# A hybrid decoder trunk on one core: a new plan for the first attention with five single PSUM banks and doubled keys, weights ahead of rows in the second mixer, and shorter reciprocal roots

## The chip, the cores and the metric

The kernel runs on one core of one Trainium2 chip. The metric is the device time of one execution in microseconds (us), the median over several runs; lower is better.

## The reference

The trunk has two layers on a residual stream `h` of 1024 tokens by 1024 features, all float32. Each layer is a token mixer and a channel mixer, each behind an RMS norm and added to `h`. Layer 0 mixes tokens by forgetting attention (16 heads of 64, causal, with a cumulated log-sigmoid gate as a bias), layer 1 by native sparse attention over keys and values that are computed once from `h` after layer 0. The channel mixer is a gated MLP (1024 to 2 x 2816 to 1024) with a causal convolution of width 3.

```python
def rms_norm(x, g):
    y = xf * lax.rsqrt(jnp.mean(xf * xf, axis=-1, keepdims=True) + RMS_EPS)
    return (y * g.astype(jnp.float32)).astype(x.dtype)
...
def forgetting_attention(xn, w_in, b_f, q_gain, k_gain, w_out):
    proj = xn @ w_in
    q = rms_norm(proj[..., :HD].reshape(B, T, N_HEADS, HEAD_DIM), q_gain)
    k = rms_norm(proj[..., HD:2 * HD].reshape(B, T, N_HEADS, HEAD_DIM), k_gain)
    v = proj[..., 2 * HD:3 * HD].reshape(B, T, N_HEADS, HEAD_DIM)
    c = jnp.cumsum(log_f, axis=1).transpose(0, 2, 1)
    ...
        s = jnp.einsum('bhqd,bhkd->bhqk', qb, k) * scale
        s = s + cb[..., :, None] - c[..., None, :]
        s = jnp.where(kpos[None, :] <= qpos[:, None], s, -jnp.inf)
        p = jax.nn.softmax(s, axis=-1)
        return jnp.einsum('bhqk,bhkd->bqhd', p.astype(v.dtype), v)
    ...
    return o @ w_out
...
    for layer in range(DEPTH):
        if layer < N_A_LAYERS:
            h = h + forgetting_attention(rms_norm(h, a_norm[i]), ...)
        else:
            h = h + native_sparse_attention(rms_norm(h, b_norm[i]), positions, kc, vc, ks, vs, kw, vw, ...)
        h = h + conv_ffn(rms_norm(h, f_norm[layer]), f_w_up[layer], f_conv_w[layer], f_conv_b[layer], f_w_down[layer])
        if layer == N_A_LAYERS - 1:
            kv = shared_kv(h, positions, ...)
```

## The kernel before

Matmuls run on operands that are split in a high and a low part (`_h`, `_l`, 128 x 512 pieces): ACT casts the high part, DVE or POOL subtracts it from the source for the low part (lines L894 and L895, L1102 and L1098), and a product is three matmuls (L220, L221, L222: high by high, low by high, high by low).

The stages, in order of time: input projections of layer 0 (to about 247 us); the first attention (to about 612 us); the rest of its output projection (648); the first mixer, `ffn0` (1291); the inputs of the second attention, `nsa_in` (1470); the second attention, `nsa` (2008); the second mixer, `ffn1`.

Within a stage each engine works its instructions off in the order of the program. That order is set when the program is built, by a planner (`Flow`): each step is a task with an engine, an estimated duration, a due time `u` and a letter; the table `PLAN` gives each letter a shift of its due time. The planner simulates the engines with the estimated durations and takes at each point the ready task that is due first. A `ready` holds a task back to a time on the planner's clock. A ring is a set of buffers that tasks take and give back.

A step of the first attention, for a head and one or two tiles of 128 queries: PE multiplies queries by keys into a score tile (L627, `s`); DVE reads it, adds the mask and finds the maximum (L635, `pt`, `sm`); ACT takes the exponential (L637); DVE inverts the row's sum (L640); POOL scales the row (L641); PE transposes blocks of 128 (L654, `t`); ACT casts the high part (L665, `p_h`); DVE subtracts for the low part (L667, `p_l`); PE multiplies by the values (L659, L660, `v`). Between these stand the late products (queries, keys and values of the second half of the heads, for the last four tiles; products of `w_h`, `wo_h` and `w_raw` into `t`), the loads and splits of the output weights (`wo_h`, `wo_l`, from `w_raw<-in_a_w_out`), and an early part of the output projection.

PSUM's eight banks are given out so in this stage: three single ones to the ring `t`, four to the ring `s` (two score tiles of two banks), one to `v`:

```python
        ring("t", 3, [P, 512], FT, space=PSUM, ordered=False)
        ring("s", 2, [P, T], FT, space=PSUM)
        ring("v", 1, [P, 512], FT, space=PSUM)
```

Queries and keys go through DRAM. A key tile is stored as 64 rows high and 64 rows low for each head (`s_k`, L494 and L762), and loaded as `ka` (the high rows twice, by two DMAs of 64 rows) and `kb` (the low rows and two rows of the gate, L802). All these DMAs are issued by SP, in order.

An RMS norm's reciprocal root is five DVE operations around two of ACT (L253 `tensor_scalar`, L245 `Ln`, L246 `Exp`, L249 to L252 one Newton step). In `ffn0` the function `leave` takes each finished row tile: square with sum (ACT, L2228), root, scaling on POOL (L2231), transposes.

At the start of `ffn1` three last row tiles are loaded, squared (L1170), scaled on POOL (L1172) and transposed (L1183), while the first weights are cast (L1102) and their lows are subtracted on DVE (L1098).

Of the kernel before, what the change touches and what calls it, by code (L numbers as in the profile page):

```python
# [16 lines left out]
P = 128  # L17
# [33 lines left out]
def moved(*shape):  # L51
# [5 lines left out]
    "fox": dict(F=1e3, G=-11.5, R=.5, M=5, E=-1, K=-.5, H=-1.5, L=-5.5, V=2, J=-4, D=1.5, N=18.5, Q=1.5, W=13, P=-3, S=0, O=1, spread=.7, wo=.6, wo_from=21, side=2, late=2, step=1.6, gap=.015),  # L57
# [3 lines left out]
    "nsa": dict(D=18.5, E=28, F=40.5, G=42.5, H=3, J=17, K=19, L=-5.5, M=20, N=-11.5, O=15, P=19.5, Q=6.5, R=20, S=-1, V=28.5, W=25.5, none=18.5, spread=0.3, wo=3, wo_from=2, side=2, cmp=0.5, gap=0.05, load=1.2),  # L61
# [40 lines left out]
class Flow:  # L102
# [3 lines left out]
    def __init__(self, plan):  # L106
        self.plan, self.rings, self.tasks = plan, {}, []
# [41 lines left out]
    def run(self):  # L149
        free = {t.eng: 0.0 for t in self.tasks}  # L150
# [46 lines left out]
class Trunk:  # L197
# [34 lines left out]
    def rstd(self, pool, ss, n, inv, p=P):  # L232
        steps, r = self.rstd_steps(pool, ss, n, inv, p)
        for f in steps:
            f()
        return r

    def rstd_steps(self, pool, ss, n, inv, p=P, room=None):
# [5 lines left out]
        def root():  # L244
            nc.scalar.activation(y, v, AF.Ln)  # L245
            nc.scalar.activation(y, y, AF.Exp, scale=-0.5)  # L246

        def correct():
            nc.vector.tensor_mul(t, y, y)  # L249
            nc.vector.tensor_mul(t, t, v)  # L250
            nc.vector.tensor_scalar(t, t, -0.5, 1.5, op0=OP.mult, op1=OP.add)
            nc.vector.tensor_mul(r, y, t)  # L252
        return (lambda: nc.vector.tensor_scalar(v, ss, inv, EPS, op0=OP.mult, op1=OP.add), root, correct), r  # L253

    def rstd_tasks(self, ss, n, inv, scale, room=lambda: None):
# [3 lines left out]
        def begin():  # L259
            st["f"], st["r"] = self.rstd_steps(self.ap_o, ss(), n, inv, room=room())  # L260
            st["f"][0]()

        def end():
            st["f"][2]()
            scale(st["r"])
        return [("DVE", .08, "Q", begin), ("ACT", .36, "Q", lambda: st["f"][1]()), ("DVE", 1.42, "Q", end)]
# [33 lines left out]
    def zeros(self, cp):  # L300
        nc = self.nc
        one_zero = cp.tile([P, 2], FT, name="one_zero")
        self.one, self.zero = one_zero[:, :1], one_zero[:, 1:]
# [118 lines left out]
    def fox_in(self, cp, xT, qT, kT, vS, extras, room):  # L422
        nc, A = self.nc, self.A
        w_in = A["a_w_in"][0]
        with self.pool("fi_s", 2) as sp, self.pool("fi_w", 2) as wp, \
# [12 lines left out]
            def gate():  # L438
# [37 lines left out]
                for x, c in enumerate((ch, cl)):  # L476
                    nc.sync.dma_start(kT[:, :, 2 * HD + x, :].rearrange("p a t -> (p a) t"), f32(c))

            def spill(o, dst, half, i, gain):
# [12 lines left out]
                for x, t in enumerate((hi, lo)):  # L492
                    for a in range(2):
                        nc.sync.dma_start(dst[4 * half:4 * half + 4, a, x * HD:(x + 1) * HD, tl].rearrange("p d t -> d p t"),  # L494
                                          f32(t[a * HD:(a + 1) * HD]))
# [1841 lines left out]
```

## Time and profile before

| | |
|---|---|
| median of 3 runs | 2655.86 us (2654.89 to 2657.86) |
| profiled execution | 2656.26 us, span 2654.5 us |
| busy PE / PEld / DVE | 2590.8 (98%) / 2165.1 (82%) / 2158.6 (81%) |
| busy ACT / POOL | 1523.1 (57%) / 541.6 (20%) |
| DMA | 310.80 MB, mean 117 GB/s |

Busy times are sums over the span and can hide in one engine's wait for another; PE's records overlap, since a matmul is started before the last one has ended. The stage is what the profile is read by.

### The profile page before, as it was taken

How to read it: one execution, taken by the hardware profiler on the slowest of the kernel's cores; microseconds unless marked ns; L12 is line 12 of the kernel's file. 1: busy time of each engine (PE TensorE's matmuls, PEld its weight loads, DVE VectorE, ACT ScalarE, POOL GpSimd, SP SyncE). 2: the span in 40 equal slices, each digit the busy share in tenths (PEclk: the TensorE clock that was granted, in tenths of full speed). 3: DMA queues.
4: the chain of work that ended last, by engine and by line, in shares of the span. 5: the costliest groups of instructions: out<-in, count | busy, mean ns of one | idle time of the engine just before them, and what ended most of it. 6: DMA issues, size and time to landing. Idle time of an engine off the chain costs nothing.

```text
span 2654.5 us, 38676 instructions
## 1 busy us (share of the span) xinstructions
PE 2590.8 (98%) x12936; PEld 2165.1 (82%) x12936; DVE 2158.6 (81%) x4471; ACT 1523.1 (57%) x3168; POOL 541.6 (20%) x846
## 2 busy tenths in 40 slices
PE   8999998899999999999999999999999999999999
PEld 6778877787888888888898788888887788888887
DVE  7763778766987877889888899988997988786988
ACT  5332777655554545444674687777875545454443
POOL 1001445420000000000354564444551000000000
PEclk9999999999999999999999999999999999999999
DMA  6474656723422222735324410000124322225553
GB/s 184 112 200 159 175 160 202 193 83 128 135 80 96 72 96 81 280 109 166 110 91 111 120 56 16 30 33 32 47 71 136 124 94 74 94 72 182 181 173 131
DMA packets 276775, 310.80 MB, mean 117 GB/s; under 512 B 19944, under 2 KB 194448, under 8 KB 276576
## 3 DMA queue, kind: packets, MB, share of 16 engines
q1 hardware_dynamic: 276144, 306.76, 37.2%
q8 instruction: 102, 1.67, 0.3%
q10 hardware_dynamic: 432, 1.57, 0.2%
q14 instruction: 97, 0.79, 0.1%
HBM read 236.84 MB, written 71.43 MB: 116 GB/s over the span
## 4 chain that ended last, share of the span: by engine, by line
PE 78%; DVE 14%; ACT 3%; issue 2%; DMA 1%; POOL 1%; SPq 0%; DVEq 0%; ACTq 0%; POOLq 0%
PE ps L221 15%; PE ps L222 15%; PE ps L220 15%; PE s L627 6%; PE t L654 5%; PE v L659 3%; PE v L660 3%; PE ps_m L220 3%; PE ps_m L222 2%; PE ps_m L221 2%; PE t L220 2%; PE t L222 2%; PE t L221 2%; DVE op L1098 2%; DVE sum L1098 1%
## 5 line engine op out<-in xcount | busy, mean ns | idle before, releaser
L1102 ACT CAST op<-sum 128x512 fp32r<-128x512 f32 x396 | 239.9, 622 | 401.1 <-PE ps L222 281.9
L220 PE MATMUL ps<-xs,op 128*128 128x512 f32 x880 | 342.7, 389 | 2.9 <-DVE u L1098 2.7
L221 PE MATMUL ps<-xs,op 128*128 128x512 f32 x880 | 342.5, 389 | 0.1
L222 PE MATMUL ps<-xs,op 128*128 128x512 f32 x880 | 342.4, 389 | 0.0
L1098 DVE TENSOR_TENSOR op<-sum,op 128x512 fp32r<-128x512 f32 x396 | 266.7, 689 | 83.1 <-ACT op L1102 82.6
L637 ACT ACTIVATE pt<-pt,sm 128x640 f32<-128x640 f32 (+7 forms) x384 | 288.1, 752 | 47.4 <-DVE sm L635 44.9
L667 DVE TENSOR_TENSOR p_l<-t,p_h 128x512 fp32r<-128x512 f32 x456 | 276.3, 630 | 41.9 <-ACT p_h L665 39.6
L665 ACT CAST p_h<-t 128x512 fp32r<-128x512 f32 x456 | 234.8, 539 | 103.1 <-PE t L654 100.9
L654 PE MATMUL t<-ident,pt 128*128 128x128 f32 x1632 | 241.8, 276 | 18.4 <-DVE p_l L667 11.9
L221 PE MATMUL ps<-op 128*128 128x512 f32 x616 | 240.3, 390 | 1.9 <-DVE op L1098 1.8
L654 PEld LDWEIGHTS t<-ident,pt 128*128 128x128 f32 x1632 | 195.6, 142 | 55.5 <-DVE p_l L667 16.5
L220 PE MATMUL ps<-op 128*128 128x512 f32 x616 | 240.2, 390 | 0.0
L222 PE MATMUL ps<-op 128*128 128x512 f32 x616 | 239.7, 389 | 0.0
L641 POOL TENSOR_SCALAR pt<-pt,sm,gate 128x640 f32<-128x640 f32 (+7 forms) x256 | 200.8, 792 | 151.3 <-DVE sm L640 101.7
L1311 DVE SCALAR_TENSOR_TENSOR acc<-u,conv,acc 128x1023 f32<-128x1023 f32 (+1 forms) x176 | 225.6, 1282 | 4.4 <-ACT acc L1312 1.5
L220 PEld LDWEIGHTS ps<-xs,op 128*128 128x128 f32 x880 | 165.2, 188 | 38.6 <-DVE u L1098 2.1
L221 PEld LDWEIGHTS ps<-xs,op 128*128 128x128 f32 x880 | 165.2, 188 | 34.7 <-DVE xs L1098 0.6
L222 PEld LDWEIGHTS ps<-xs,op 128*128 128x128 f32 x880 | 165.2, 188 | 34.2
L635 DVE CUSTOM_DVE_ANT_0 pt<-s,mask 128x128 f32<-128x128 f32 (+7 forms) x256 | 153.2, 614 | 19.4 <-PE t L654 9.8
L659 PE MATMUL v<-p_h,v 128*128 128x512 f32 (+1 forms) x376 | 152.7, 408 | 2.1 <-DVE o_early L683 1.4
L1102 ACT CAST op<-w_raw 128x512 fp32r<-128x512 f32 x132 | 81.5, 624 | 104.8 <-PE ps L222 103.9
L2231 POOL TENSOR_SCALAR h<-h,nt_rs 128x1024 f32<-128x1024 f32 x8 | 10.0, 1258 | 631.2 <-DVE nt_rs L252 612.2
(501 smaller groups left out, 6375.2 us busy)
## 6 DMA issues: line engine op xcount, KB each, us to landing
w_raw<-in_f_w_up SPq DMA_DIRECT2D x96, 512.0 KB
u<-in_f_w_down SPq DMA_DIRECT2D x176, 256.0 KB
s_g<-acc SPq DMA_DIRECT2D x40, 512.0 KB
g<-s_g SPq DMA_DIRECT2D x20, 1024.0 KB
w_raw<-in_a_w_in SPq DMA_DIRECT2D x32, 512.0 KB
qa<-s_q SPq DMA_DIRECT2D x32, 256.0 KB
ka<-s_k SPq DMA_DIRECT2D x32, 256.0 KB
v<-s_v SPq DMA_DIRECT2D x16, 512.0 KB
```

Source lines behind the costliest of these rows:

```text
L220: mm(out, a[0], b[0], start=start, stop=False, **kw)
L221: mm(out, a[0], b[1], start=False, stop=False, **kw)
L222: mm(out, a[1], b[0], start=False, stop=stop, **kw)
L637: e = F.add("ACT", .238 + .8333e-3 * n, u, "E", lambda c=c, out=out: nc.scalar.activation(out(), out(), AF.Exp, bias=sm["nm"][:, c], scale ...
L641: ("POOL", (.327 if gate else .24) + .8333e-3 * n, "N", lambda r=r, c=c, out=out: nc.gpsimd.tensor_scalar(out(), out(), sm["rs"][:, c], ga ...
L654: nc.tensor.transpose(t.t[:, r * P:(r + 1) * P], b(), self.ident)
L659: nc.tensor.matmul(out, v(), p2.t[0][:, :n], start=first, stop=False)
L665: h = F.add("ACT", .052 + .8333e-3 * n, u + 1 + x, "H", lambda: nc.scalar.copy(p2.t[0][:, :n], t.t[:, :n]), after=[a], uses=[t, p2])
L667: lambda: nc.vector.tensor_tensor(p2.t[1][:, :n], t.t[:, :n], f32(p2.t[0][:, :n]), op=OP.subtract), after=[h], uses=[t, p2])
L1098: TT = lambda out, a, b, op: nc.vector.tensor_tensor(out, a, b, op=op)
L1102: a = F.add("ACT", .53, u, "A", lambda: nc.scalar.copy(op.t[:, 0], src()), after, [op], uses)
L1311: return lambda: nc.vector.scalar_tensor_tensor(acc.t[:, sh:], o.t[:, :T - sh], cw[j][:, c:c + 1], acc.t[:, sh:], op0=OP.mult, op1=OP.add)
```

## The change

It has five parts.

1. The first attention gets a new table for its order. Each late product (`late`), each load of an output weight (`wo`) and each row tile of the early output projection (`row`) now has a due time of its own; loads count 1.2 times as long. The ring `t` has five banks and the ring `s` one tile. A product of the output projection waits for the one weight it needs and no longer for all, and a weight's split waits for one step of the last late product.
2. The high rows of a key are stored twice in DRAM, so that `ka` is one DMA of 128 rows: six store DMAs for a key tile where there were four, and two load DMAs where there were three.
3. A root takes `Ln` with scale and bias directly from the sum, with -0.5 times the argument computed beside it on DVE, and the Newton step in three operations (four for several columns, counted with that one).
4. In `ffn0`, `leave` takes the root of four row tiles at once. In `nsa_in` five small rows are loaded later.
5. In `ffn1`, the planner's clock for DVE begins at 8.4, the first weights may come 2 earlier, and the lows of the first three operands go to POOL.

The table for `nsa` changes also; its order hardly does.

```diff
 PLAN = {
-    "fox": dict(F=1e3, G=-11.5, R=.5, M=5, ..., step=1.6, wo=.6, wo_from=21, side=2, late=2, gap=.015),
+    "fox": dict(D=13.5, E=35.5, F=109.5, G=4.5, ...,
+                late=[-102.2, -25, 10.2, ...], wo=[143.8, -146, 79.8, ...], row=[91, 7.5, 19.5, 23, 240.5],
+                spread=.7, side=2, gap=.015, load=1.2),
...
         def root():
-            nc.scalar.activation(y, v, AF.Ln)
+            nc.scalar.activation(y, ss, AF.Ln, scale=inv, bias=self.eps[:p])
             nc.scalar.activation(y, y, AF.Exp, scale=-0.5)
 
         def correct():
-            nc.vector.tensor_mul(t, y, y)
-            nc.vector.tensor_mul(t, t, v)
-            nc.vector.tensor_scalar(t, t, -0.5, 1.5, op0=OP.mult, op1=OP.add)
-            nc.vector.tensor_mul(r, y, t)
+            if n == 1:
+                nc.vector.scalar_tensor_tensor(t, y, y, v, op0=OP.mult, op1=OP.mult)
+            else:
+                nc.vector.tensor_mul(t, y, y)
+                nc.vector.tensor_mul(t, t, v)
+            nc.vector.scalar_tensor_tensor(r, t, 1.5, y, op0=OP.add, op1=OP.mult)
...
-        ring("t", 3, [P, 512], FT, space=PSUM, ordered=False)
-        ring("s", 2, [P, T], FT, space=PSUM)
+        ring("t", banks, [P, 512], FT, space=PSUM, ordered=False)
+        ring("s", (7 - banks) // 2, [P, T], FT, space=PSUM)
...
+                self.store_pairs(dst[4 * half:4 * half + 4, :, :, tl], (hi, lo) if gain is None else (hi, hi, lo))
...
-                        loaded_k = load(u, k_there, kb, *[(lambda x=x, n=n, kb=kb: kb.t[0][x * HD:(x + 1) * HD, :n], kT[p, a, :HD, :n]) for x in range(2)],
-                                        (lambda n=n, kb=kb: kb.t[1][:, :n], kT[p, a, HD:, :n]))
+                        loaded_k = load(u, k_there, kb, (lambda n=n, kb=kb: kb.t[0][:, :n], kT[p, a, :P, :n]), (lambda n=n, kb=kb: kb.t[1][:, :n], kT[p, a, P:, :n]))
...
-            def split_op(u, src, op, after, uses, ready=0.0):
+            def split_op(u, src, op, after, uses, ready=0.0, tail="DVE"):
...
+                eng, dur, tt = ("DVE", .6, nc.vector) if tail == "DVE" else ("POOL", 1.25, nc.gpsimd)
+                return F.add(eng, dur, u, "B", lambda: tt.tensor_tensor(op.t[:, 1], src(), f32(op.t[:, 0]), op=sub), [a], uses=[op, *uses])
...
             BEFORE = 8.0 if layer else 3.0
+            if layer:
+                F.begin["DVE"] = BEFORE + .4
...
-                ready = split_op(u - (40 if f < AHEAD and m < 2 else 4), src, op, after, uses, BEFORE - 3.0 if u < 6 else 0.0)
+                ready = split_op(u - (40 if f < AHEAD and m < 2 else 4), src, op, after, uses, BEFORE - (5.0 if layer else 3.0) if u < 6 else 0.0,
+                                 "POOL" if layer and u < 3 else "DVE")
...
+            F.add("SP", 3.0, -5, "", small_rows).ready = 7.0
```

PE in the first attention, before: two score groups of four matmuls each stand together (names as above).

```order
L659 MATMUL v<-p_h,v 128x128
L660 MATMUL v<-p_l,v 128x128
L627 MATMUL s<-ka,qa 128x512
L627 MATMUL s<-kb,qb_80 128x512
L627 MATMUL s<-ka,qa 128x256
L627 MATMUL s<-kb,qb_80 128x256
L627 MATMUL s<-ka,qa 128x512
L627 MATMUL s<-kb,qb_80 128x512
L627 MATMUL s<-ka,qa 128x384
L627 MATMUL s<-kb,qb_80 128x384
```

PE around the same place of the first attention, after (lines are shifted by 3 or 4):

```order
L663 MATMUL v<-p_h,v 128x128
L664 MATMUL v<-p_l,v 128x128
L223 MATMUL t<-w_h,wo_h 128x512
L224 MATMUL t<-w_l,wo_h 128x512
L225 MATMUL t<-w_h,wo_l 128x512
L631 MATMUL s<-ka,qa 128x512
L631 MATMUL s<-kb,qb_80 128x512
L631 MATMUL s<-ka,qa 128x256
L631 MATMUL s<-kb,qb_80 128x256
L658 MATMUL t<-ident,pt_3901 128x128
L223 MATMUL t<-w_h,wo_h 128x512
L224 MATMUL t<-w_l,wo_h 128x512
```

A score group now has products or transposes ahead of it and behind it; before, there are ten places with two groups in one piece, after there is none.

ACT in the first attention, before, where casts of output weights (`wo_h`) stand between casts of probabilities:

```order
L637 ACTIVATE pt_5018,sm<-pt_5018,sm 128x256
L894 CAST wo_h<-w_raw 128x512 x2
L665 CAST p_h<-t 128x128
L894 CAST wo_h<-w_raw 128x512
L665 CAST p_h<-t 128x512
L637 ACTIVATE pt_5069,sm<-pt_5069,sm 128x384
```

ACT there after:

```order
L641 ACTIVATE pt_5075,sm<-pt_5075,sm 128x128
L904 CAST wo_h<-w_raw 128x512 x2
L669 CAST p_h<-t 128x128
L641 ACTIVATE pt_5098,sm<-pt_5098,sm 128x256
L641 ACTIVATE pt_5130,sm<-pt_5130,sm 128x384
L669 CAST p_h<-t 128x512
```

The next cast of a weight comes some ten rows later instead of one row later: the casts of a weight stand in a pair, and the pairs stand further apart.

PE at the start of the second mixer, before (`o_h` the second attention's output, `ident` the transposes, `op` the first weight operand; the number behind a name is a buffer's):

```order
L221 MATMUL t<-wo_l,o_h 128x512
L222 MATMUL t<-wo_h,o_l 128x512
L1183 MATMUL ps<-ident,u 128x128 x8
L220 MATMUL ps<-xT_u_20193,op 128x512
L221 MATMUL ps<-xT_u_20194,op 128x512
```

PE there after:

```order
L224 MATMUL t<-wo_l,o_h 128x512
L225 MATMUL t<-wo_h,o_l 128x512
L223 MATMUL ps<-xT_u_20051,op 128x512
L224 MATMUL ps<-xT_u_20052,op 128x512
L225 MATMUL ps<-xT_u_20051,op 128x512
```

The transposes of the loaded rows, which came directly behind the output projection, now come behind 24 matmuls of the mixer.

SP at the start of the second attention's inputs, before (`w_raw` weights, `s_h` the rows that are stored):

```order
L2224 DMA s_h_72<-h_10871 128x1024 x2
L312 DMA bg<-in_b_b_gate 128x48
L312 DMA g_kc<-in_kc_gain 128x64
L312 DMA g_ks<-in_ks_gain 128x64
L312 DMA g_kw<-in_kw_gain 128x64
L312 DMA g_r<-in_b_q_gain 128x16
L1625 DMA w_raw<-in_b_w_in 128x2x24
L1625 DMA w_raw<-in_kv_w 128x2x384
```

SP there after:

```order
L1644 DMA w_raw<-in_kv_w 128x2x384
L1644 DMA w_raw<-in_b_w_in 128x2x24
L2267 DMA s_h_72<-h_10695 128x1024 x2
L2267 DMA s_h_72<-h_10820 128x1024 x2
L1593 DMA bg<-in_b_b_gate 128x48
L1593 DMA g_kc<-in_kc_gain 128x64
L1593 DMA g_ks<-in_ks_gain 128x64
L1593 DMA g_kw<-in_kw_gain 128x64
L1593 DMA g_r<-in_b_q_gain 128x16
L1644 DMA w_raw<-in_kv_w 128x2x384
```

The `w_raw<-in_b_w_in` piece that stood behind the five small rows now stands ahead of them and of the last four stores.

More of the change, by code (lines that the diff above doesn't have):

```diff
@@ L700, in late_tasks @@
         stored = [[], [], []]
-        u = plan["late"]
+        order = iter(plan["late"])
+        u = next(order)
         def quarter(kind, c):
@@ L2131, in nsa_attn, with leave_row, turn, head @@
             self.run(F)
+    def leave_row(self, F, i, h, d, u, turns, xn, normed_half):
+        nc = self.nc
+        if i < 4:
+            turns.append((i, h))
+            return
+        for c in (0, 4):
+            ps = F.buf("ps")
+            def turn(ps=ps, c=c):
+                for k in range(4):
+                    nc.tensor.transpose(ps.t[:, k * P:(k + 1) * P], h()[:, (c + k) * P:(c + k + 1) * P], self.ident)
+            a = F.add("PE", .43, u, "g", turn, [d], [ps])
+            four = lambda ps=ps: ps.t.rearrange("p (k t) -> p k t", t=P)
+            def head(c=c, four=four):
+                normed_half(1)
+                nc.scalar.copy(self.xcol(xn, 0, i, c, 4), four())
+            def rest(c=c, four=four):
+                nc.vector.tensor_tensor(self.xcol(xn, 1, i, c, 4), four(), f32(self.xcol(xn, 0, i, c, 4)), op=OP.subtract)
+            F.chain(u, [("ACT", .48, "h", head), ("DVE", .6, "r", rest)], [a], uses=[ps])
     def kv_tiles(self, p, U):
@@ L2226, in square @@
                 def square():
-                    st["rs"] = self.ap_o.tile([P, 5, 1], FT, name="nt_rs")
-                    nc.scalar.activation(junk.t, h(), AF.Square, accum_out=st["rs"][:, 0])
-                *steps, last = self.rstd_tasks(lambda: st["rs"][:, 0], 1, 1.0 / D, lambda r: st.update(r=r), lambda: st["rs"][:, 1:])
-                d = F.chain(u, [("ACT", 1.05, "e", square), *[(*x[:2], "e", x[3]) for x in steps], ("DVE", .5, "e", last[3])], [*after, self.after_silu], [junk])
-                d = F.add("POOL", 1.28, u, "e", lambda: nc.gpsimd.tensor_scalar(h(), h(), st["r"], 1.0, op0=OP.mult, op1=OP.mult), [d, stored])
@@ new lines, in square @@
+                    nc.scalar.activation(junk.t, h(), AF.Square, accum_out=four_rows["rs"][:, 0, i % 4:i % 4 + 1])
+                four_rows.setdefault(i // 4, []).append((F.add("ACT", 1.05, u, "e", square, [*after, self.after_silu, *[a for a, *_ in four_rows.get(i // 4, [])[:1]]], [junk]), h, stored))
+                if i % 4 < 3:
+                    return
+                *steps, last = self.rstd_tasks(lambda: four_rows["rs"][:, 0], 4, 1.0 / D, lambda r: four_rows.update(r=r), lambda: four_rows["rs"][:, 1:])
@@ L2252, in ahead @@
+                d = F.chain(u, [*[(*x[:2], "e", x[3]) for x in steps], ("DVE", .6, "e", last[3])], [a for a, *_ in four_rows[i // 4]])
+                for k, (_, h, stored) in enumerate(four_rows[i // 4]):
+                    self.leave_row(F, i - 3 + k, h, F.add("POOL", 1.28, u, "e", lambda h=h, k=k: nc.gpsimd.tensor_scalar(
+                        h(), h(), four_rows["r"][:, k:k + 1], 1.0, op0=OP.mult, op1=OP.mult), [d, stored]), u, turns, xn, normed_half)
             def ahead(F, u):
```

119 lines of the change are left out of this document (57 added, 62 removed).

## The prediction

> **What bounds the kernel now.** I read the busy table by stages first, then the first attention in 20 us slices, its waits and groups, and last the timeline where the waits stand. Columns of the first two fences: stretch, length, busy time (instructions) of PE, PEld, DVE, ACT and POOL, granted clock, DMA share, GB/s.
>
> ```profile
> 1478.00:2010.00 532.00, 521.20 (x3159) 445.67 (x3157) 473.08 (x1324) 409.01 (x968) 279.67 (x370) 1.00 0.16 51
> 2010.00:2654.50 644.50, 636.48 (x2804) 525.18 (x2804) 549.13 (x787) 321.77 (x523) 6.42 (x4) 0.99 0.38 125
> sum 2654.50, PE 2590.80 PEld 2165.07 DVE 2158.62 ACT 1523.08 POOL 541.59; mean PE 370.11 PEld 309.30 DVE 308.37 ACT 217.58 POOL 77.37
> ```
>
> PE is the bound: its records leave 2654.50 - 2590.80 = 63.7 us. The diff removes almost no matmul, so it can only win where PE stands still or runs at a lower clock. The second attention leaves 10.8 us and the second mixer 8.0; the first attention more:
>
> ```profile
> 300.00:320.00 20.00, 18.32 (x103) 15.34 (x102) 13.59 (x41) 17.18 (x42) 16.77 (x18) 1.00 0.78 218
> 360.00:380.00 20.00, 17.33 (x96) 14.94 (x95) 17.03 (x46) 14.36 (x36) 11.59 (x13) 0.91 0.69 208
> 420.00:440.00 20.00, 15.28 (x92) 12.72 (x91) 18.85 (x51) 16.15 (x42) 10.04 (x12) 0.99 0.55 164
> 440.00:460.00 20.00, 18.42 (x110) 15.95 (x108) 17.41 (x53) 17.77 (x43) 13.37 (x16) 0.92 0.77 229
> 460.00:480.00 20.00, 12.94 (x68) 10.57 (x67) 11.90 (x31) 13.78 (x33) 13.35 (x14) 0.85 1.00 249
> 480.00:500.00 20.00, 18.48 (x115) 16.04 (x114) 17.68 (x43) 17.53 (x36) 8.77 (x10) 0.98 0.74 212
> sum 364.00, PE 341.16 PEld 288.42 DVE 266.93 ACT 243.59 POOL 139.86; mean PE 18.95 PEld 16.02 DVE 14.83 ACT 13.53 POOL 7.77
> ```
>
> The sum is that of 247 to 611 us. PE idles there for 364 - 341.16 = 22.8 us, and the granted clock costs about (0.09 + 0.01 + 0.08 + 0.15 + 0.02) x 20 = 7 us more: some 30 us are lost at least. The four slices from 420 to 500 us hold 4.7 + 1.6 + 7.1 + 1.5 = 14.9 idle and 5.2 clock, 20 of the 30. A busy record can also be a matmul that started late, so I count the work at the pitch of an undisturbed piece:
>
> ```profile
> 282.02 0.40 PE L627 MATMUL s<-ka,qa 128*128 128x512 f32 x1
> 282.26 0.39 PE L627 MATMUL s<-kb,qb 66*128 66x512 f32 x1
> 282.95 0.71 PE L654 MATMUL t<-ident,pt 128*128 128x128 f32 x5
> 283.42 0.31 PE L627 MATMUL s<-ka,qa 128*128 128x128 f32 x1
> ```
> ```profile
> L654 PE MATMUL t<-ident,pt 128*128 128x128 f32 x576 | 91.4, 279 | 13.7 <-DVE p_l L667 9.6 <-DVE w_raw L742 3.3 <-DVE ohl_l L754 0.4
> L220 PE MATMUL t<-wo_h,ohl_h 128*128 128x512 f32 x75 | 29.9, 399 | 0.2 <-DVE p_l L667 0.2
> L635 DVE CUSTOM_DVE_ANT_0 pt<-s,mask 128x896 f32<-128x896 f32 (+6 forms) x128 | 94.9, 748 | 17.7 <-PE t L654 8.9 <-PE s L627 7.1 <-POOL pt L641 1.0
> ```
>
> A matmul of 512 columns starts every 0.235 us and a transpose every 0.47/5 = 0.094. There are 576 blocks of 128 keys by 128 queries; each has one transpose, two score matmuls and two value matmuls of 128 columns (0.059 each): 576 x (0.094 + 4 x 0.059) = 190 us. The products of this stretch are 3 x 75 of the early out-projection and, by the program, 12 late ones of 24 matmuls: 513 x 0.235 = 121. With some 40 other transposes (4 us) about 315 us of work stand in 364, so 49 us are lost. This upper count and the lower one of 30 bound what a new order can win here.
>
> ```profile
> PE t L654 <- DVE p_l L667: 9.6, 7, 4.3
> PE s L627 <- DVE sm L635: 2.9, 5, 1.4
> ACT wo_h L894 <- DMA w_raw<-in_a_w_out: 5.1, 1, 5.1
> ```
> ```profile
> 468.51 0.61 ACT L665 CAST p_h<-t 128x512 fp32r<-128x512 f32 x1
> 474.23 0.62 ACT L894 CAST wo_h<-w_raw 128x512 fp32r<-128x512 f32 x1 [5.11 <-DMA w_raw<-in_a_w_out]
> 476.11 0.48 PE L654 MATMUL t<-ident,pt 128*128 128x128 f32 x1 [4.28 <-DVE p_l L667]
> ```
> ```profile
> 459.73 1.28 POOL wo_l L895
> 463.68 10.53 DMA w_raw<-in_a_w_out
> ```
>
> The largest wait (columns: total, times, longest) is put down to DVE's p_l, but the reader sees who is behind it: ACT, in order, stands 5.11 us at a cast of an output weight whose load has not landed; the probability casts behind it, their lows on DVE and PE's transposes stand with it. The chain of waits has that load with 10.53 us, in the slice where DMA is busy throughout (1.00, 249 GB/s). Just before, the chain runs over POOL, which splits such weights (1.28 us each) ahead of the row scalings that the transposes need. That stretch is also the one where, in the order before, no late product stands between the attention's steps.
>
> **The change, part by part.**
>
> New order, five single banks, one score tile. No PE work is added. In the new order the output-weight casts stand in pairs between more exponentials and score groups are evenly spread: at ten places before, two groups stand together; after, none do. By the two orders and the pitches above, the other PE work between neighbouring groups runs from 0 to 6.65 us before and from 1.13 to 2.85 after, median 2.0. Five banks let PE run two transposes or products further ahead of ACT and DVE. The loads of output weights are counted longer by the planner and spread: from the first to the last, they no longer end with a burst of seven casts. Against it: with one score tile the next group waits until DVE has read this one, 0.75 us mean (94.9/128) plus two handovers, for which I count 0.15 us each (an estimate on the long side: POOL's rows end at 2011.27 and PE starts at 2011.33 in a fence below). Against the gaps of the new order that is short at 8 of 96 groups, 3.8 us in all, if DVE comes at once. What stands ahead of the read on DVE can add to it; DVE is 266.93/364 = 73% busy, so a read finds an operation of about 0.6 us in progress in most groups, some 0.25 us mean, which the median slack 2.0 - 1.05 covers. And the filler-free piece is not gone: 48 us of PE work without a late product (32 before), in which ACT and DVE carry nearly as much as PE. So I take 14 of the 20 us from 420 to 500 us, 5 of the 10 elsewhere, 5 of the 19 that only the count shows, and give back 4: -20. Bounds: -33 (30 recovered, and a few of the hidden), +5 (the load stall moves elsewhere and the eight short groups stay).
>
> Doubled keys.
>
> ```profile
> L494 SPq DMA_DIRECT2D s_k<-sp_h x24: 574/600/617, 97.3 to 191.5; - x24
> L802 SPq DMA_DIRECT2D ka<-s_k x48: 444/588/1465, 150.7 to 525.9; - x48
> ```
>
> The high part is stored twice: 24 + 8 stores more, 32 x 0.60 = 19 us of SP, 24 x 0.60 = 14 of it in the projections, and 4 MB more written. Of 48 loads 24 go: 24 x 0.59 = 14 us of SP less, with the same bytes. SP's stores in the projections stand ahead of weight loads, each up to 1.2 us later per tile; PE there works from weights that were loaded before. I take +1 (0 to +4), the upper end if three rows come late by such a pair.
>
> Second mixer's start.
>
> ```profile
> 2000.61 0.38 SPq L1219 DMA_DIRECT2D w_raw<-in_f_w_up  x1
> 2007.47 0.39 PE L222 MATMUL t<-wo_h,o_l 128*128 128x512 f32 x1
> 2010.15 1.12 POOL L1172 TENSOR_SCALAR u<-u,nt_rs 128x1024 f32<-128x1024 f32 x1 [12.79 <-DVE nt_rs L250]
> 2010.37 0.90 DVE L252 TENSOR_TENSOR nt_rs<-nt_rs 128x1 f32<-128x1 f32 x1
> 2011.33 1.97 PE L1183 MATMUL ps<-ident,u 128*128 128x128 f32 x8 [3.47 <-POOL u L1172]
> 2012.94 0.78 PE L220 MATMUL ps<-xT_u,op 128*128 128x512 f32 x1
> 2013.52 0.63 PE L221 MATMUL ps<-xT_u,op 128*128 128x512 f32 x1
> 2016.81 0.40 PE L220 MATMUL ps<-xT_u,op 128*128 128x512 f32 x1
> ```
>
> PE ends the out-projection at 2007.86, waits 3.47 us for the last row's root and scaling, then works slowly: nine matmuls start between 2012.94 and 2016.81, 0.43 us each where 0.235 is the pitch, 1.8 us lost, and the transposes' piece loses about 0.7: 6 us in all. After the change PE has 24 matmuls (5.6 us) ahead of the first transposes, on rows that were turned long before; the last of their weights was issued at 2000.61, ACT casts the first ahead of its squares, and POOL makes the first three lows, so the gap of 3.47 us is covered. If that cover fails, the same root is waited for as before. But DVE is 549.13/644.5 = 85% busy in this stage and nearer to full at its start, and what PE starts early it meets again there: I take -4.5 (-6.5 to -1).
>
> Against POOL as the place of the lows speaks the Trainium skill, "SBUF — State Buffer", section "Who interferes with whom": DVE and GpSimd take turns at one pair of ports, and who comes second is held for the whole instruction. The rows agree in one case: the DVE operation at 2010.37 lasts 0.90 us and ends with POOL's at 2011.27. By that rule three lows of 1.28 us could hold DVE for 3.8 us, and this term would be -0.7 instead of -4.5. Since POOL's three stand ahead of the roots and mostly beside DVE's wait for the last product, I keep -4.5.
>
> Roots, batches, small rows at the second attention's input.
>
> ```profile
> PE ps L1602 <- DVE xT L1548: 3.5, 2, 2.9
> 1305.89 0.31 ACT L1633 ACTIVATE w_h<-w_raw,g_b 128x24 fp32r<-128x24 f32 x1 [5.89 <-DMA w_raw<-in_b_w_in]
> 1297.29 0.78 SPq L312 DMA_DIRECT2D bg<-in_b_b_gate  x1
> 1301.22 0.38 SPq L1625 DMA_DIRECT2D w_raw<-in_b_w_in  x1
> ```
>
> ACT waits 5.89 us for a load that SP issues only after five small rows (1297.29 to 1301.22, 3.9 us). In the new order it stands ahead of them, so the load can come up to 3.9 us earlier, and behind ACT's casts PE's 3.5 us go. Late instead are the rows of the last four tiles: their roots wait for the fourth square, and their transposes come one product later; the gate bias still comes behind the stores. I take -2 (-5 to +2). In the other 90 or so roots one or two DVE operations of 0.15 to 0.17 us go, and ACT no longer waits for one. Nearly all of these lie beside PE's work; the cover is the product that PE has in hand, and without it each is worth 0.3 us. I take -0.5 at the kernel's start (-2 to 0). The second attention's order is nearly unchanged; a tenth of its 10.8 idle: -1 (-4 to +3).
>
> Sum: -20 + 1 - 4.5 - 2 - 0.5 - 1 = -27. The profiled execution took 2656.26 us (span 2654.5, 1.8 around it), 0.4 above the median of 2655.86: about 2629.
>
> **The rivals.** One score tile ties PE to DVE. Place: the 96 groups of the first attention, where already with two tiles PE waited 2.9 us for the read. Price: every group whose read is queued behind a low or a weight's split on DVE keeps PE, in order, from all that follows. The other terms and the better order are worth 31 us without my 4 for this, so it decides from 31/96 = 0.32 us a group; at 0.5 it costs 48 and the time is 2656 + 48 - 31 = 2673. For it speaks the filler-free piece, where DVE is at 17 to 19 of 20 us; against it the median gap of 2.0 us. The Trainium skill, "Perfetto Trace Analysis", section "Optimization Strategy", says that gaps which repeat on the engine that should be saturated can mean too little SBUF or PSUM for the next tile, which would be this case; the five short waits above are the only trace of it.
>
> The stall moves: the output-weight loads still find a full DMA (0.74 to 1.00 from 440 to 500 us, and 1 MB more of stores comes before it), and ACT waits elsewhere. Then the first attention gains nothing and the boundaries remain: 2656 - 7 = 2649.
>
> Nearly everything goes: 28 of the 30 visible and 6 of the 19 hidden us, with the boundaries: 2656 - 34 - 7 = 2615.
>
> **How the numbers follow.** Forecast, the first attention 12 to 28 us shorter: 0.62. Nearly everything: 0.14. The stall moves: 0.14, of which 0.08 ends still faster by over 0.2% and 0.06 within (0.2% is 5.3 us, about what these measurements can tell). Score tile decides: 0.10. So faster 0.84, same 0.06, slower 0.10. The range goes from 2608, below the third rival, to 2651, above the second; outside lie the slow case and about 0.07 at the ends.
>
> **What would show it.** Right: in the slices from 420 to 500 us PE is busy for over 18 of 20 at a clock above 0.95, and no cast of an output weight waits over 2 us; after the out-projection PE goes on without a gap of 3 us; ACT no longer waits for the load of 1305.89. Wrong: PE waiting for DVE's score read in many small pieces, over 30 us in all; or ACT at another load in the first attention; or a longer projection stage.

## The result and the profile after

| | before | changed |
|---|---|---|
| median, same comparison (5 runs each) | 2657.11 us (2654.89 to 2657.86) | 2644.41 us (2639.51 to 2647.94) |
| profiled execution | 2656.26 us | 2647.94 us, 3.5 above its median |

The ratio is 0.9949 (95% interval 0.9933 to 0.9966): 12.7 us faster, a little under half of the 27 that the sum gave. The direction was right, 2644 lies in the range, and 2629 was too low. By the table below the input projections came out 10.5 us worse than the sum had them and the second mixer 9.4, with the wrong sign; 5.6 us behind the first attention were not in the sum; three other stages gained 2 us more each than forecast.

Where it went, by the time at which the same event comes in the two profiled executions (us):

| event | before | changed | difference | this stage | forecast |
|---|---|---|---|---|---|
| first score matmul of the first attention | 253.2 | 264.3 | +11.0 | +11.0 | +0.5 |
| end of the early output projection | 614.8 | 603.6 | -11.2 | -22.2 | -20 |
| end of the rest of that projection | 654.0 | 648.4 | -5.6 | +5.6 | 0 |
| last transposes at the second attention's inputs | 1312.5 | 1302.5 | -9.9 | -4.3 | -2 |
| end of the second attention | 2007.9 | 1994.7 | -13.2 | -3.3 | -1 |
| last row transposed in the second mixer | 2031.2 | 2019.3 | -11.9 | +1.3 | -4.5 |
| end | 2654.5 | 2646.2 | -8.3 | +3.6 | |

Two of these boundaries do not part the same work. Before, ten matmuls of the rest of the projection (`o_rows`) stand among the early ones:

```profile
602.64 0.39 PE L220 MATMUL ps_m<-wo_h,o_rows 128*128 128x512 f32 x1
602.97 0.50 PE L220 MATMUL t<-wo_h,ohl_h 128*128 128x512 f32 x1
```

Changed, all of them come behind the early ones, and three matmuls of a late product come ahead of the first score matmul instead of behind it. At 0.23 us each that moves 2.3 and 0.7 us from one stage to another: for the same work the first three rows are +10.3, -19.2 and +3.3.

The first attention, changed, in the slices of the prediction (same columns: stretch, length, PE, PEld, DVE, ACT, POOL, clock, DMA share, GB/s):

```profile
420.00:440.00 20.00, 19.90 (x123) 16.88 (x122) 18.34 (x52) 15.79 (x40) 5.93 (x8) 1.00 0.62 167
440.00:460.00 20.00, 16.99 (x92) 14.08 (x91) 17.71 (x54) 17.96 (x45) 12.60 (x15) 0.91 0.77 246
460.00:480.00 20.00, 15.60 (x83) 12.62 (x82) 14.10 (x37) 13.78 (x33) 9.51 (x12) 0.91 0.85 234
480.00:500.00 20.00, 19.95 (x121) 17.15 (x120) 17.61 (x39) 19.07 (x41) 14.84 (x14) 1.00 0.77 246
```

PE idles 7.6 us in them where it idled 14.9. The filler-free piece still loses (440 to 480 us), as the order had it. PE's longest waits in the whole stage, changed (what waits, for what: total, times, longest):

```profile
PE t L761 <- DVE w_raw L754: 3.2, 2, 1.9
PE s L631 <- DVE sm L639: 1.8, 5, 0.6
PE s L631 <- DVE p_l L671: 1.4, 1, 1.4
PE s L631 <- DMA ka<-s_k: 1.0, 1, 1.0
```

The 4.28 us behind the weight's load are gone, and the single score tile costs 1.8 us in five waits, 3.2 if the one put down to `p_l` is also for the tile.

What the prediction did not see begins earlier. Changed, in the input projections, where PE before was busy for 20.00 of 20 in each slice from 140 us on:

```profile
140.00:160.00 20.00, 15.94 (x72) 12.21 (x71) 10.36 (x25) 7.24 (x13) 0.00 (x0) 0.97 0.80 218
160.00:180.00 20.00, 20.00 (x90) 15.64 (x90) 10.97 (x30) 6.55 (x14) 0.00 (x0) 0.94 0.68 164
180.00:200.00 20.00, 16.07 (x69) 12.75 (x69) 10.54 (x21) 7.69 (x12) 0.00 (x0) 0.91 0.82 213
```
```profile
PE ps_t L328 <- DMA col_in<-in_vc_pe: 3.9, 1, 3.9
PE ps_t L328 <- DMA col_in<-in_f_conv_w: 2.5, 1, 2.5
PE ps_t L328 <- DVE sp_l L230: 1.5, 1, 1.5
```

SP's queue and PE there, changed, from the timeline (start, length, engine, line, operation):

```profile
183.25 2.57 SPq L698 DMA_DIRECT2D s_k<-sp_h  x4
185.91 1.25 SPq L698 DMA_DIRECT2D s_k<-sp_l  x2
187.26 0.55 SPq L326 DMA_DIRECT2D col_in<-in_vc_pe  x1
189.33 0.20 PE L328 MATMUL ps_t<-ident,col_in 16*128 16x16 f32 x1 [3.93 <-DMA col_in<-in_vc_pe]
```

`col_in` are small column vectors (convolution weights, gains) that PE transposes between the products of the projections. Their loads stand in SP's queue behind a key tile's stores. With six stores the load of `vc_pe` came behind a second tile's stores, and PE, in order, stood until it had landed. The same load before and changed (count: shortest, median and longest issue, first and last start):

```profile
L319 SPq DMA_DIRECT2D col_in<-in_vc_pe x1: 354/354/354, 175.6 to 175.6; - x1
L326 SPq DMA_DIRECT2D col_in<-in_vc_pe x1: 553/553/553, 187.3 to 187.3; - x1
```

### The profile page after: what moved, and what is told of

It reads as the page before. It is cut to its first block, busy times and chain, and to the rows that moved or that the text cites. A ratio compares the mean times of both kernels' runs of the same rounds, so it can differ in the third digit from the quotient of the medians.

```text
span 2646.2 us, 38548 instructions
## 1 busy us (share of the span) xinstructions
PE 2590.0 (98%) x12936; PEld 2167.0 (82%) x12936; DVE 2135.0 (81%) x4323; ACT 1527.2 (58%) x3156; POOL 542.2 (20%) x849
## 4 chain that ended last, share of the span: by engine, by line
PE 62%; DVE 9%; ACT 2%; issue 1%; DMA 1%; POOL 0%; SPq 0%; DVEq 0%; ACTq 0%; POOLq 0%
PE ps L224 15%; PE ps L225 15%; PE ps L223 15%; PE s L631 4%; PE t L658 4%; PE v L663 2%; PE v L664 2%; DVE op L1116 2%; DVE sum L1109 1%; PE t L223 1%; PE t L225 1%; PE t L224 1%; DVE pt L639 1%; DVE b L1109 1%; DVE xs L1109 1%
## 5 line engine op out<-in xcount | busy, mean ns | idle before, releaser
L658 PE MATMUL t<-ident,pt 128*128 128x128 f32 x1632 | 234.8, 274 | 1.7 <-DVE w_raw L1563 0.8
```

What stands on the lines that cost most here:

```text
L658: nc.tensor.transpose(t.t[:, r * P:(r + 1) * P], b(), self.ident)
```

## The experiments

Each is compared with the kernel before on the same chip; times are medians. The medians of before in these comparisons run from 2654.9 to 2658.7 us, so rows of different comparisons can be told apart to a few us only. A single profile can be further off: that of e11_one is 4.6 us over its median, and its first attention, the same program as e1_single's, took 6.9 us longer. The experiments with the changed kernel as a base differ from it by the edit alone.

| run | median, us | to before, us | ratio, 95% interval |
|---|---|---|---|
| changed | 2644.41 | -12.7 | 0.9949 (0.9933 to 0.9966) |
| e1_single | 2637.83 | -17.1 | 0.9937 (0.9925 to 0.9950) |
| e2_cols | 2639.33 | -15.6 | 0.9942 (0.9930 to 0.9955) |
| e3_lows_dve | 2643.40 | -11.5 | 0.9963 (0.9951 to 0.9976) |
| e4_mixer_old | 2643.26 | -11.7 | 0.9957 (0.9943 to 0.9970) |
| e5_feed | 2645.40 | -11.2 | 0.9960 (0.9945 to 0.9975) |
| e6_new_3banks | 2696.99 | +40.4 | 1.0151 (1.0134 to 1.0168) |
| e7_old_5banks | 2699.92 | +43.3 | 1.0169 (1.0149 to 1.0189) |
| e8_old_3banks | 2667.23 | +10.6 | 1.0041 (1.0026 to 1.0056) |
| e9_turns_first | 2633.52 | -24.7 | 0.9909 (0.9895 to 0.9923) |
| e10_unbatched | 2646.04 | -12.2 | 0.9951 (0.9939 to 0.9964) |
| e11_one | 2638.50 | -19.7 | 0.9926 (0.9914 to 0.9939) |
| e12_old | 2633.66 | -24.6 | 0.9911 (0.9896 to 0.9926) |
| e13_quarters | 2645.82 | -12.9 | 0.9952 (0.9935 to 0.9969) |
| e14_before_quarters | 2653.04 | -5.7 | 0.9977 (0.9967 to 0.9987) |
| e15_before_doubled | 2668.69 | +10.0 | 1.0036 (1.0024 to 1.0049) |
| e16_both | 2647.83 | -8.0 | 0.9968 (0.9954 to 0.9981) |
| e17_fox_roots | 2638.85 | -17.0 | 0.9936 (0.9919 to 0.9952) |

### Doubled keys

e1_single, keys stored once (the planner's estimate for the loads is kept, so the order stays):

```diff
-                self.store_pairs(dst[4 * half:4 * half + 4, :, :, tl], (hi, lo) if gain is None else (hi, hi, lo))
+                self.store_pairs(dst[4 * half:4 * half + 4, :, :, tl], (hi, lo))
...
-                        loaded_k = load(u, k_there, kb, (lambda n=n, kb=kb: kb.t[0][:, :n], kT[p, a, :P, :n]), ...)
+                        loaded_k = load(u, k_there, kb, *[(lambda x=x, n=n, kb=kb: kb.t[0][x * HD:(x + 1) * HD, :n], kT[p, a, :HD, :n]) for x in range(2)], ...)
```

> The changed kernel with the high rows of a key stored once again (four stores for a key tile, three loads), PE's order unchanged. Theory A, the doubled stores hold SP and with it the small column loads that PE's transposes in the projections wait for (9 us between 130 and 200 us, with the lower clock 11): these waits go, the stage from 130 to 230 us is 9 to 11 us shorter, and the time is about 2634 us. Rival B, the projections are longer for another reason (the shorter roots, other DVE order), and the extra key load costs SP 14 us in the first attention: within 3 us of the changed kernel, 2641 to 2648.

Measured: 4.4 us more of a gain than the changed kernel's, where theory A expected about 10; in the profile PE waits for nothing between 100 and 260 us. The slices of e1_single:

```profile
140.00:160.00 20.00, 20.00 (x94) 15.38 (x93) 13.03 (x31) 9.31 (x17) 0.00 (x0) 1.00 0.77 202
180.00:200.00 20.00, 20.00 (x94) 16.53 (x93) 8.10 (x16) 5.46 (x9) 0.00 (x0) 1.00 0.87 240
```

The first score matmul comes at 252.5 us, 11.8 ahead of the changed kernel's; 2.7 of it go back in the first attention. That is theory A by the place. The medians differ by 4 to 7 us and not by 11: the changed kernel's runs spread over 8.4 us, and its profiled one is the longest of them.

e2_cols, doubled keys kept, each column load asked for four columns ahead (the loop alone is shown):

```diff
-                    cols[name] = self.columns(sp, pp, ap, k, o)
+                    fetch(n + 4)
+                    cols[name] = self.columns(raws[n], pp, k, o)
```

> The changed kernel with the doubled stores kept, but each small column load asked for four columns ahead of its transpose. Theory A, position in SP's queue: the waits for the column loads go, about 2635 us. Rival C, traffic: the 4 MB of extra stores make every load of that stage late, those of the weights too, so PE waits for other loads instead and the time stays over 2640.

```profile
PE ps_m L223 <- ACT w_h L229: 2.3, 2, 1.4
PE ps_m L224 <- DVE w_l L230: 1.2, 2, 0.8
```

Measured 2639.3 us, between the two expectations. The column waits are gone and nearly half of the loss with them: the first score matmul comes 5.0 us earlier than in the changed kernel. For the rest, PE now waits for casts of weights that were late, as rival C has it. But the loads of weights stand behind the doubled stores in SP's queue too, and the DMA engines were no busier here than before (0.78 of the time from 140 to 160 us, 0.84 before), so this run does not tell traffic from position.

e15_before_doubled, the kernel before with doubled keys alone:

```diff
-                for x, t in enumerate((hi, lo)):
+                for x, t in enumerate((hi, lo) if gain is None else (hi, hi, lo)):
```

> The kernel before with doubled keys alone (stores and loads; some 40 rows of PE's order move). If the stores hold the column loads here as in the changed kernel: the projections are 8 to 11 us longer, and the first attention's loads are 24 DMAs fewer, 2660 to 2668. If the 11 us need the changed kernel's other parts: within 3 us of before.

Measured +10.0 us, with the same kind of wait. In its profile the first score matmul comes 14.8 us later, more than the 8 to 11 expected, and 2.7 us come back in the first attention:

```profile
PE ps_t L321 <- DMA col_in<-in_kc_pe: 4.0, 1, 4.0
```

So this part alone costs about 10 us in the surroundings of before, where the 24 loads that it saves are worth little.

### Order and banks of the first attention

e6_new_3banks is `rooms, 3` for `rooms, 5`. e7_old_5banks takes the old due times, with the old load costs and weight waits:

```diff
+    "fox": dict(F=1e3, G=-11.5, R=.5, ..., late=[2 + 1.6 * k for k in range(12)], wo=[21 + .6 * k for k in range(8)], row=[0] * 5),
...
-        return stored, [steps[k:k + 1] for k in (1, 3, 5, 3, 3, 7, 7, 7)]
+        return stored, [after] * 8
```

e8_old_3banks is both.

> The changed kernel's due times, but the first attention with three single banks and two score tiles as before (the planner orders anew). If the order alone carries the 19 us of that stage: within 5 us of the changed kernel. If the five banks carry it: 10 us or more above, 2654 and over. If the single score tile cost PE much: under the changed kernel; by its trace (PE waits 1.8 us for the score reads) that is excluded.

> The changed kernel with five single banks and one score tile, but the first attention's due times, load costs and weight waits as before. If the banks carry the gain: 2644 to 2650. If the order does: 2656 and over, and with the old bunched score groups on one tile more than with three banks.

> The changed kernel with the first attention undone, due times and banks as before (keys still doubled). By the trace that stage and the rest of its output projection gained 19 - 5 = 14 us net, so 2655 to 2662.

| | old due times | new due times |
|---|---|---|
| three banks, two score tiles | 2667.2 | 2697.0 |
| five banks, one score tile | 2699.9 | 2644.4 |

Together they are worth 23 us in the changed kernel; each alone costs some 30. The 23 us are not the gain over the kernel before: e8, expected at 2655 to 2662, came out at 2667, and by its profile the old order and banks serve this kernel worse than they served that one. Its first attention is 6.9 us longer than before, where with doubled keys alone (e15) it is 2.7 shorter. Over the first attention and the whole output projection behind it, nearly the same work, the changed kernel gains 16 us on before. The waits of PE in this stage, e7_old_5banks first, then e6_new_3banks (two rows):

```profile
PE s L629 <- DVE sm L637: 32.0, 33, 5.5
```
```profile
PE t L223 <- ACT ohl_h L859: 13.5, 2, 12.6
PE s L631 <- DVE sm L639: 8.8, 21, 0.9
```

The first row is the rival of the prediction, in an order that did not make room for it: 33 waits for the score read, 32 us. The changed order spreads the groups and has 1.8 us of it. In e6 the new due times let the planner, with other buffers, place a product ahead of what it needs (12.6 us in one wait).

e17_fox_roots leaves only this part, the shorter roots, the second attention's numbers and, other than its expectation says, the five small rows that are loaded later.

> Only the first attention's new order and banks, the shorter roots and the second attention's numbers; keys stored once, second mixer and the second attention's inputs as before. By the stages of the trace: -19 in the first attention, +5 behind it, -1 in the second attention: 15 us under before, 2641 to 2645. If the stall at the inputs goes here too: 2635 to 2638.

Measured -17.0 us, in between. By its profile 18.7 us are gained by the end of the early output projection, 5.4 go back right behind it, the stretch from there to the end of the second attention gives 6.6, and the second mixer loses 2.0.

### The second mixer's start

e3_lows_dve (`"POOL" if layer and u < 3 else "DVE"` becomes `"DVE"`), e4_mixer_old (also without `F.begin["DVE"]`, and 3.0 for 5.0), e5_feed (7.0 for 5.0):

> The changed kernel with the first three lows of the second mixer back on DVE; casts and DVE's start in the plan as changed. Theory D: POOL's slower lows (1.5 us each) hold the weight buffers, so that the next loads, casts and DVE's lows come 3.7 us late, and DVE, which is the bound there, loses it for good: 3 to 5 us shorter than the changed kernel, 2640. Rival E: DVE is full in any case and the lost time is its own work: no difference over 1.5 us.

> The changed kernel with the start of the second mixer as before (no start for DVE in the plan, casts and lows as before). If the part gains its 3.5 us gap and keeps it, this is 4 to 5 us longer than the changed kernel (2649); if DVE gives it back, as the trace of the changed kernel has it (a gain of 5.6 us at the start, then 10 us lost by 2065 us), it is 4 to 5 us shorter (2640).

> The changed kernel with the second mixer's first four casts (both weights that are there) ahead of the squares on ACT, by a ready time 2 earlier; nothing else moves on the other engines. Theory D2: DVE stands 5.5 us at the start of that mixer because ACT casts only one operand before the squares, so the third load's buffer comes free 4 us late; with the casts ahead DVE is fed, and the time is 3 to 5 us under the changed kernel's 2644.4. Rival: the load's way (3.9 us) or the later roots take the place, and nothing changes (within 1.5 us).

None of the three differs from the changed kernel clearly. Theories D and D2 fall: with lows on DVE, or with four casts ahead, DVE's longest stand at a cast is 3.8 and 6.7 us, where it was 3.7. That the whole part can be undone without loss (e4) says that its gain is given back. The changed kernel's timeline shows the gain first, then where it goes:

```profile
1994.28 0.39 PE L225 MATMUL t<-wo_h,o_l 128*128 128x512 f32 x1
1994.51 0.39 PE L223 MATMUL ps<-xT_u,op 128*128 128x512 f32 x1
1998.01 0.38 SPq L1233 DMA_DIRECT2D w_raw<-in_f_w_up  x1
2001.21 2.19 PE L1197 MATMUL ps<-ident,u 128*128 128x128 f32 x16 [0.23 <-POOL u L1186]
2001.94 1.14 ACT L1113 CAST op<-w_raw 128x512 fp32r<-128x512 f32 x2 [3.92 <-DMA w_raw<-in_f_w_up]
2002.59 1.90 DVE L1116 TENSOR_TENSOR op<-w_raw,op 128x512 fp32r<-128x512 f32 x2 [3.70 <-ACT op L1113]
2007.19 0.68 DVE L1109 TENSOR_TENSOR b<-acc,xT_u 128x512 f32<-128x512 f32 x1
2018.20 1.09 PE L1197 MATMUL ps<-ident,u 128*128 128x128 f32 x8 [2.40 <-POOL u L1186]
```

PE goes from the projection into the mixer without a gap. But the rows are transposed 6.5 us after the projection's end instead of 3.5, and DVE comes to their sums (`b`) 12.5 us after it instead of 6.6. Ahead of them it stands for a weight whose load was issued only at 1998.01, as ACT ended the casts of the weights before it; that SP waits there for their buffer is read from the order. DVE's busy time and the clock in the first 10 us, changed, then before:

```profile
1995.00:2005.00 10.00, 9.24 (x47) 7.08 (x46) 4.47 (x13) 4.86 (x11) 6.30 (x5) 1.00 0.72 241
```
```profile
2008.00:2018.00 10.00, 6.67 (x25) 5.68 (x26) 9.11 (x23) 7.79 (x23) 4.46 (x3) 0.66 0.62 210
```

PE gains 2.6 us and the clock; DVE loses 4.6. At the start of this mixer DVE is the fuller engine and sets the pace (before):

```profile
2048.00:2073.00 25.00, 23.23 (x101) 18.60 (x101) 24.82 (x38) 13.54 (x20) 0.00 (x0) 1.00 0.60 186
```

Later PE does: from 2148 to 2248 us it is busy for all 100 us and DVE for 80. In the changed kernel PE meets DVE's loss at the rows' root (2.40 us at 2018) and at this wait, which was 1.6 us before:

```profile
PE ps L223 <- DVE u L1109: 2.9, 1, 2.9
```

Theory F was put to the chip with keys stored once (base e1_single). e9_turns_first has only the first operand ahead and no start for DVE, so that the rows' transposes come first; e11_one keeps DVE's start, and one product (12 matmuls) stands ahead; e12_old has the start wholly as before.

```diff
-                ready = split_op(..., BEFORE - (5.0 if layer else 3.0) if u < 6 else 0.0,
-                                 "POOL" if layer and u < 3 else "DVE")
+                ready = split_op(..., BEFORE - (5.0 if layer and (f, m) == (0, 0) else 3.0) if u < 6 else 0.0,
+                                 "POOL" if layer and (f, m) == (0, 0) else "DVE")
```

> Keys stored once (as in the run with single keys, 2637.8), and in the second mixer only the first weight's cast and low ahead of the rows, with no start for DVE in the plan: PE has the rows' transposes directly behind the output projection again, as before. Theory F: DVE bounds that mixer, so what counts is when the rows reach DVE, and 24 matmuls ahead of the transposes keep them from it for 6 us; PE's gap of some 3 us comes back and costs nothing in the end: 2634 to 2639. Rival: the gap is lost time as forecast, and this is 4 us or more above the run with single keys, 2642.

> Keys stored once, and in the second mixer one product (12 matmuls) instead of two ahead of the rows' transposes, its low on POOL. By theory F the rows reach DVE 3 us earlier than in the run with single keys while most of PE's gap stays covered: 2633 to 2636. If DVE's five lows ahead of the rows still wait for the third load: as with single keys, 2637 to 2639.

> Keys stored once and the second mixer's start wholly as before. By the run with that start alone undone (no difference) this is the time with single keys within 2 us, 2636 to 2640; if the new start is worth its covered gap, 2642.

The times in this table run from the end of the second attention's projection (us):

| run | PE's gap ahead of the first transposes | DVE at the first row sum | DVE idle in the first 15 us | to the kernel's end, profile | median |
|---|---|---|---|---|---|
| changed | none | 12.5 | 6.1 | 651.5 | 2644.4 |
| e4_mixer_old | 2.8 | 6.7 | 1.1 | 648.7 | 2643.3 |
| e1_single | none | 12.8 | 6.9 | 650.0 | 2637.8 |
| e11_one | none | 11.0 | 5.1 | 651.5 | 2638.5 |
| e9_turns_first | 2.7 | 5.1 | 0.9 | 647.5 | 2633.5 |
| e12_old | 2.8 | 6.7 | 1.2 | 648.3 | 2633.7 |
| before | 3.5 | 6.6 | 1.1 | 646.6 | 2657.1 |

The two rows of e9_turns_first:

```profile
1986.29 1.97 PE L1196 MATMUL ps<-ident,u 128*128 128x128 f32 x8 [2.68 <-POOL u L1185]
1988.68 1.52 DVE L1110 TENSOR_TENSOR b<-acc,xT_u 128x512 f32<-128x512 f32 x1
```

With the gap back and DVE fed the kernel is not slower: theory F holds. How much faster is less sure. The time to the kernel's end separates the two starts in every profile here: 649.2 to 652.0 us in the twelve runs with products ahead of the rows, 647.5 to 648.7 in the four with the rows first (e4, e9, e12, e17). So the new start costs about 2 us. The medians give 4 with keys stored once (7 against each comparison's own before) and nothing clear with doubled keys (e4). Part of the loss is not the start's: with the old start (e4, e12, e17) this stretch is still about 2 us longer than in the kernel before and its two variants e14 and e15 (646.1 to 646.7). What brings these was not told apart. e11_one, with one product ahead, gains nothing over e1_single: DVE still stands 4.6 us at casts that wait for the third load. e9_turns_first and e12_old are the fastest kernels here, 0.9% under before.

### The second attention's inputs

e10_unbatched (one root per row tile in `leave`, as before), e13_quarters (`c, 16.0` becomes `c` for the second weight quarters), e14_before_quarters (that ready time alone in the kernel before), e16_both (e10 and e13).

> The changed kernel with the first mixer's roots taken for each row tile as before, not for four at once. If the batch is what moved the weight load and its casts ahead at the second attention's inputs, the 7 us gained there go back: 2649 to 2652. If the 7 us have another cause (shorter roots, late quarters): within 2 us of 2644.

> The changed kernel without the ready time of 16 for the second weight quarters at the second attention's inputs (PE's order is unchanged; two casts and two lows of weights go back ahead of the rows' casts on ACT and DVE). If this place in ACT's order is the cause of the 7 us: ACT stands 5 us at the load again, 2649 to 2652. If not: 2643 to 2646.

> The kernel before with that ready time alone; it moves the four casts behind the rows' and nothing else. If it is the cause: PE's waits of 2.9 and 0.6 us and the lower clock behind them go, 5 to 7 us under before, 2649 to 2652. If it takes the batch as well: within 2 us of before.

> The changed kernel with both undone at the second attention's inputs, the batched roots and the ready time of 16. If either suffices to keep ACT from standing at the load, undoing both brings the stall back: 2649 to 2652. If neither is the cause: 2643 to 2647.

Undoing either edit alone gives nothing back. Made alone in the kernel before, the ready time gives 5.7 us by the medians and 2.8 in this stretch of the profile. Undoing both costs 2 to 5 us by the medians (2647.8, between the two expectations), and the interval of e16 overlaps those of e10 and e13. So each seems to be enough for most of the gain, which is why the first two looked like no cause. PE's wait there in the changed kernel, and ACT's in e16_both, for 5.89 us before:

```profile
PE ps L224 <- DVE w_l L1657: 0.5, 1, 0.5
```
```profile
ACT w_h L1653 <- DMA w_raw<-in_b_w_in: 2.1, 1, 2.1
```

ACT's stand is not all back in e16_both, and SP's queue there gives a likely reason: the edit leaves the five small rows late.

```profile
1289.63 0.50 SPq L1644 DMA_DIRECT2D w_raw<-in_b_w_in  x1
1290.18 0.46 SPq L1593 DMA_DIRECT2D bg<-in_b_b_gate  x1
1293.09 0.32 ACT L1653 ACTIVATE w_h<-w_raw,g_b 128x24 fp32r<-128x24 f32 x1 [2.15 <-DMA w_raw<-in_b_w_in]
```

The load stands ahead of the small rows, where before it stood behind them (1301.22). This is the mechanism that the prediction named. With it and the shorter roots alone, the stretch up to the last transposes is 2.6 us shorter than before (e16) and 2.3 (e17), against 4.3 in the changed kernel; no run puts the small rows back. A part of what the expectations call 7 us is that one execution of before: in e15_before_doubled, with the same order there, PE's wait for the rows (`xT`) is 0.9 us and not 3.5.

## Why the prediction was right or wrong

Of the prediction's four signs of being right, three came true: no cast of an output weight waits over 0.7 us, PE goes on without a gap of 3 us behind the second attention's projection, and ACT's 5.89 us are gone. The fourth, PE busy over 18 of 20 us at a clock above 0.95 from 420 to 500 us, came true in half: from 440 to 480 us it is busy for 17.0 and 15.6 of 20 us at a clock of 0.91. Of its signs of being wrong one came true, a longer projection stage.

**The first attention (-20).** Right in size, and in mechanism with the places shifted. For the same work the stage became 19 us shorter in the profile. PE's idle time fell from 22.9 to 9.3 us and the clock's loss (counted as in the prediction) from 7.0 to 3.6: 17 us that a profile shows, some 2 more that only the count shows. Of the 20 us from 420 to 500 us 9 came back, not 14; elsewhere 8, not 5. That the total fits is in part luck. The load stall is gone, the filler-free piece is not, and the single tile costs 1.8 to 3.2 us, under the 4 given back.

**One score tile as a rival (0.10).** Not what happened, but its price was real: in the old order it is 32 us of waits (e7). The count of groups that were short of room in the new order was the row that decided.

**Doubled keys (+1, to +4).** The step that failed most: +11 in the profile's projections, +10 for this part measured alone (e15), and 4 to 7 by the medians when it is taken out of the changed kernel (e1). The prediction counted 14 us more of SP in the projections and said that PE works there from weights loaded before. It did not look for what else PE takes from SP there: the column loads behind those stores, which PE's order has between the products. Their row would have been in the trace of before, as transposes of `col_in` every 6.4 us. And where the columns came in time (e2), PE waited for weights after all.

**Second mixer's start (-4.5).** Wrong in sign: +1.3 by the last row's transposes and +4.9 by the end, of which about 2 to 3 are this part's and the others stay with the old start. The gap went as said. What failed is the step that puts 24 matmuls ahead of the first transposes because their own rows were turned long before: the three rows behind them are DVE's work, DVE sets the pace there, and 24 matmuls in front of their transposes let it stand 5.5 us. The prediction saw that PE meets DVE's load again, and priced it at 1.5 of 6 us. The rule from the Trainium skill, "SBUF — State Buffer", section "Who interferes with whom", by which POOL's lows could hold DVE, would have come nearer (-0.7), but for another reason than the one measured: beside POOL's lows from 1997.06 to 2000.05 us no operation of DVE lasts over 0.84 us, and with the lows on DVE (e3) nothing was gained.

**Inputs of the second attention (-2).** Right in direction and, as far as the runs go, in mechanism: 4.3 us by the profile, of which 2.3 to 2.6 are there when little but the load ahead of the small rows is left (e16, e17). That the later ready time of the second quarters moves two casts of weights behind the rows' casts, and alone also takes most of the stall away (e14), was not read from the order.

**Not in the sum: behind the first attention (+5.6).** 2.3 us of it are the ten matmuls that moved here; 3.3 are lost. The last early row tile now ends the stage, and its store and reload stand behind a load that SP issued just before. Changed:

```profile
603.04 0.33 SPq L986 DMA_DIRECT2D h_rows<-in_x  x1
604.40 0.32 SPq L898 DMA_DIRECT2D s_h<-w_raw  x1
609.52 0.32 SPq L1019 DMA_DIRECT2D h_rows<-s_h  x1
616.62 1.97 PE L1005 MATMUL ps_t<-ident,h_rows 128*128 128x128 f32 x8 [2.53 <-POOL h_rows L1001]
```

Before, that reload was issued 2.6 us after the store (615.60 to 618.20), now 5.1 after, and PE waits 3.6 us in two pieces for rows (1.3 before). The loss comes with the new order: with the old one (e8) this stretch is no longer than before. That the load is the cause is read from the trace alone; no run here moved it.

With the two terms that failed undone (e9, e12) the kernel takes 2633.5 us, 4 from the predicted 2629. That closeness is in part luck: what is lost behind the first attention and in the second mixer with its old start was not in the sum, and larger gains at the inputs and in the second attention make up for it.

## What to carry to other kernels

When a step adds issues to a queue, list everything that stands behind it in that queue in the same stretch and who waits for each of them in order; the small loads count: here PE stood 3.9 us for one of 8 KB. Where one engine bounds a stage, a gap on another engine is worth only what it brings forward for the first: before covering PE's gap, ask when the bounding engine gets its first work. And an order and the buffers it was made for are one edit: half of it can cost more than the whole brings.

## What was not expected of the hardware

A small load costs PE its whole way: `col_in` of 16 rows was issued at 187.26 and PE started at 189.33, 2.1 us for 8 KB. The three waits of 3.9, 2.5 and 1.5 us come to 7.9 of the 11 us; the granted clock of 0.97, 0.94 and 0.91 in the three slices of 20 us is worth another 3.6 by the prediction's count, so some 3 us of the loss are the clock's.
